# The down projection of a hybrid encoder layer: nine of 22 k-pairs with seven block products in place of eight

## The chip, the core and the metric

The kernel runs on one core of a Trainium2 chip. The metric is device time in microseconds (us) for one execution of the whole layer, and the comparison is between two kernels that compute the same layer.

## What is computed

One encoder layer over 256 tokens of 2048 channels, in float32: a windowed attention and a gated linear attention side by side, an output projection, and then a feed-forward part with a depthwise convolution of three taps. The change touches the last product alone, the one with `w_down`.

```python
D_MODEL, SEQ, D_FF = 2048, 256, 5632
def conv_gated_ffn(h, w_up, conv_w, conv_b, w_down):
    u = h @ w_up                                      # 256 x 11264
    up_ = jnp.pad(u, ((0, 0), (1, 1), (0, 0)))
    u = up_[:, :-2] * conv_w[0] + up_[:, 1:-1] * conv_w[1] + up_[:, 2:] * conv_w[2] + conv_b
    gate, val = jnp.split(u, 2, axis=-1)
    return (jax.nn.silu(gate) * val) @ w_down         # 256 x 5632 by 5632 x 2048
x = x + conv_gated_ffn(rms_norm(x, norm2_g), w_up, conv_w, conv_b, w_down)
```

## The kernel before

Every product of float32 numbers is made of three matmuls. A number is split into a rounded part (`hi`, type fp32r) and the residue (`lo`), and `hi*hi + hi*lo + lo*hi` is summed in PSUM. The activations are split once and stay in SBUF. The weights come from HBM unit by unit: `weights` (L104) loads 128x1024 numbers on SyncE's queue, ScalarE rounds them (L110) and VectorE subtracts to get the residue (L111). One unit is two k tiles of 128 rows by 512 output columns, and feeds 12 matmuls: two k tiles, two halves of 128 tokens, three matmuls each. The rings have four buffers for raw weights, four for `hi` and three for `lo`.

The program is recorded by a scheduler that fixes the order on every engine beforehand. An engine takes its instructions strictly in that order.

The up projection runs 22 chunks of eight units (`up`, L666). Each chunk's result leaves PSUM, is turned by a DMA, and goes through the convolution (`convolve`, L704) on VectorE and ScalarE while TensorE is already on later chunks; `behind` (L696) sets after which unit. So the convolution of the last two chunks, 20 and 21, runs while the down projection has begun. Their results are the split activations `gts`, 44 k tiles or 22 pairs of them.

The down projection (L733 to L761) takes the output columns in four blocks of 512. Each block runs over the 22 pairs, one unit a pair, into two PSUM banks (`pd`, one for each half of the tokens): 4 x 22 x 12 = 1056 matmuls. At the end of a block VectorE adds the two banks to `x1`, the input of the layer's last addition, and a DMA stores them. VectorE's residue of a unit has to wait until TensorE has let go of the `lo` buffer of three units before.

GpSimd has almost nothing to do before: twelve powers of a few columns (`inv_sqrt`, L188) and no work in the down projection.

Of the kernel before, what the change touches and what calls it, by code (L numbers as in the profile page):

```python
# [43 lines left out]
]  # L44

# [15 lines left out]
def tile_hymba_layer(  # L61
# [25 lines left out]
    def arena(shape, dt, name):  # L87
        return ar.tile(shape, dt, name=name, tag="ar")
# [644 lines left out]
    first = 0  # L733
    for c in range(4):
        ps = [acc(f"pd{c}{t}") for t in range(2)]
        for u in range(NFF // 2):
            hi, lo = weights(wd, first, 1024, f"d{c}{u}")
            if c == 0:
                behind(4 * NFF + u)
            first += P * 1024  # L740
            order = [(k, t) for k in range(2) for t in range(2)]
            if u == NFF // 2 - 1:
                order.sort(key=lambda o: o[1])
            for k, t in order:
                kt = 2 * u + k
                gt = gts[kt // 4]
                a = gt[:, 0, kt % 4, t * P : t * P + P]
                b = gt[:, 1, kt % 4, t * P : t * P + P]
                wh, wl = hi[:, k * 512 : k * 512 + 512], lo[:, k * 512 : k * 512 + 512]
                PE.matmul(ps[t], a, wh, start=(kt == 0), stop=False)  # L750
                PE.matmul(ps[t], a, wl, start=False, stop=False)  # L751
                PE.matmul(ps[t], b, wh, start=False, stop=(kt == NFF - 1))  # L752
        x1c = x1[c // 2][:, c % 2]
        for t in range(2):
            pieces = 2 if (c, t) == (3, 1) else 1
            w = 512 // pieces
            for i in range(pieces):
                sl = slice(i * w, i * w + w)
                V.tensor_tensor(x1c[:, t, sl], ps[t][:, sl], x1c[:, t, sl], ALU.add)
                q = nc.scalar if i == 0 and pieces == 2 else nc.sync  # L760
                q.dma_start(out=out[t * P : t * P + P, c * 512 + i * w : c * 512 + i * w + w], in_=x1c[:, t, sl])  # L761
# [106 lines left out]
```

## Time and profile before

| | us |
|---|---|
| median of 3 runs | 1063.92 (1063.69 to 1065.83) |
| the profiled execution, its own time | 1065.21 |
| its span, first to last instruction | 1063.4 |
| TensorE matmul busy | 1055.9 (99%) |
| VectorE busy | 703.7 (66%) |
| ScalarE busy | 581.7 (55%) |
| GpSimd busy | 15.2 (1%) |

The busy time of TensorE counts every moment in which some matmul is in flight. Matmuls overlap, so the distance between two starts is shorter than the length of one. The profiled execution's time holds 1.8 us outside its span. Its mean granted TensorE clock was 1.000, the full 2.4 GHz.

### The profile page before, as it was taken

How to read it: one execution, taken by the hardware profiler on the slowest of the kernel's cores; microseconds unless marked ns; L12 is line 12 of the kernel's file. 1: busy time of each engine (PE TensorE's matmuls, PEld its weight loads, DVE VectorE, ACT ScalarE, POOL GpSimd, SP SyncE). 2: the span in 40 equal slices, each digit the busy share in tenths (PEclk: the TensorE clock that was granted, in tenths of full speed). 3: DMA queues.
4: the chain of work that ended last, by engine and by line, in shares of the span. 5: the costliest groups of instructions: out<-in, count | busy, mean ns of one | idle time of the engine just before them, and what ended most of it. 6: DMA issues, size and time to landing. Idle time of an engine off the chain costs nothing.

```text
span 1063.4 us, 13494 instructions
## 1 busy us (share of the span) xinstructions
PE 1055.9 (99%) x4892; PEld 880.4 (83%) x4892; DVE 703.7 (66%) x957; ACT 581.7 (55%) x803; POOL 15.2 (1%) x16
## 2 busy tenths in 40 slices
PE   9999999999999999999999999999999999999998
PEld 7789888888888888888888888888888888888887
DVE  6598786755555567777777777777777755444543
ACT  6745686764445455656556565656556544433342
POOL 0021000010000000000000000000000000000000
PEclk9999999999999999999999999999999999999999
DMA  8955754346656797787887887788778767676762
GB/s 257 372 166 160 224 165 137 119 138 180 198 185 223 194 251 215 216 211 226 221 216 214 213 224 219 216 211 227 219 216 214 208 194 215 194 210 193 215 196 81
DMA packets 104706, 216.76 MB, mean 204 GB/s; under 512 B 53056, under 2 KB 53568, under 8 KB 104640
## 3 DMA queue, kind: packets, MB, share of 16 engines
q1 hardware_dynamic: 57888, 204.23, 62.8%
q10 hardware_dynamic: 46752, 11.68, 7.8%
q8 instruction: 38, 0.62, 0.2%
q14 instruction: 28, 0.23, 0.1%
HBM read 202.25 MB, written 2.10 MB: 192 GB/s over the span
## 4 chain that ended last, share of the span: by engine, by line
PE 95%; DMA 3%; DVE 1%; ACT 1%; issue 0%; DVEq 0%; SPq 0%; ACTq 0%
PE pu L678 15%; PE pu L677 15%; PE pu L679 15%; PE pd L752 8%; PE pd L750 7%; PE pd L751 7%; PE po L634 2%; PE po L635 2%; PE po L633 2%; PE pgt L259 1%; PE pqa L260 1%; PE pvg L260 1%; PE pvg L261 1%; PE pgt L261 1%; PE pgt L260 1%; PE pvg L259 1%
## 5 line engine op out<-in xcount | busy, mean ns | idle before, releaser
L111 DVE TENSOR_TENSOR lu<-ru,hu 128x1024 fp32r<-128x1024 f32 x176 | 215.1, 1222 | 124.8 <-PE pu L678 68.0
L679 PE MATMUL pu<-hu,xs 128*128 128x512 f32 x704 | 274.1, 389 | 0.0
L678 PE MATMUL pu<-lu,xs 128*128 128x512 f32 x704 | 273.9, 389 | 0.0
L677 PE MATMUL pu<-hu,xs 128*128 128x512 f32 x704 | 267.2, 389 | 0.0
L110 ACT ACTIVATE hu<-ru 128x1024 fp32r<-128x1024 f32 x176 | 186.8, 1061 | 145.7 <-PE pu L679 97.7
L111 DVE TENSOR_TENSOR ld<-rd,hd 128x1024 fp32r<-128x1024 f32 x88 | 107.7, 1224 | 112.5 <-PE pd L751 103.4
L110 ACT ACTIVATE hd<-rd 128x1024 fp32r<-128x1024 f32 x88 | 93.6, 1064 | 133.6 <-PE pd L752 128.2
L677 PEld LDWEIGHTS pu<-hu,xs 128*128 128x128 f32 x704 | 132.1, 188 | 27.5
L678 PEld LDWEIGHTS pu<-lu,xs 128*128 128x128 f32 x704 | 132.1, 188 | 27.4
L679 PEld LDWEIGHTS pu<-hu,xs 128*128 128x128 f32 x704 | 132.2, 188 | 27.4
L751 PE MATMUL pd<-ld,g 128*128 128x512 f32 x352 | 136.9, 389 | 0.0
L752 PE MATMUL pd<-hd,g 128*128 128x512 f32 x352 | 136.9, 389 | 0.0
L750 PE MATMUL pd<-hd,g 128*128 128x512 f32 x352 | 136.3, 389 | 0.0
L751 PEld LDWEIGHTS pd<-ld,g 128*128 128x128 f32 x352 | 66.1, 188 | 13.8
L752 PEld LDWEIGHTS pd<-hd,g 128*128 128x128 f32 x352 | 66.1, 188 | 13.7
L750 PEld LDWEIGHTS pd<-hd,g 128*128 128x128 f32 x352 | 66.1, 188 | 13.7
L111 DVE TENSOR_TENSOR lo<-ro,ho 128x1024 fp32r<-128x1024 f32 x32 | 38.8, 1223 | 39.0 <-ACT ho L110 29.1
L715 ACT ACTIVATE c<-v,prm_sb 128x256 f32<-128x256 f32 x88 | 48.2, 595 | 22.7 <-DVE c L719 19.5
L110 ACT ACTIVATE ho<-ro 128x1024 fp32r<-128x1024 f32 x32 | 33.9, 1060 | 46.9 <-DMA ro<-in_wo_dram 26.8
L716 DVE SCALAR_TENSOR_TENSOR c<-v,prm_sb,c 128x255 f32<-128x255 f32 x88 | 40.3, 478 | 0.6 <-ACT c L715 0.6
L685 ACT ACTIVATE us<-pu,rstd 128x512 f32<-128x512 f32 x44 | 29.9, 681 | 19.6 <-PE pu L679 19.6
L719 DVE SCALAR_TENSOR_TENSOR c<-v,prm_sb,c 128x255 f32<-128x255 f32 x88 | 40.2, 477 | 0.0
(215 smaller groups left out, 1432.6 us busy)
## 6 DMA issues: line engine op xcount, KB each, us to landing
ru<-in_wu_dram SPq DMA_DIRECT2D x176, 512.0 KB, 4.3
rd<-in_wd_dram SPq DMA_DIRECT2D x88, 512.0 KB, 4.4
ro<-in_wo_dram SPq DMA_DIRECT2D x32, 512.0 KB, 3.8
riqa<-in_wi_dram SPq DMA_DIRECT2D x16, 512.0 KB, 6.2
rivg<-in_wi_dram SPq DMA_DIRECT2D x16, 512.0 KB, 4.1
rigt<-in_wi_dram SPq DMA_DIRECT2D x16, 512.0 KB, 3.6
ri<-in_wi_dram SPq DMA_DIRECT2D x16, 384.0 KB, 4.1
riqg<-in_wi_dram SPq DMA_DIRECT2D x8, 512.0 KB, 5.0
```

The lines of the kernel that those rows point to most:

```text
L110: last["ACT"] = S.activation(hi[:, :cols], r[:, :cols], AF.Copy)
L111: last["DVE"] = V.tensor_tensor(lo[:, :cols], r[:, :cols], hi[:, :cols].bitcast(F32), ALU.subtract)
L260: PE.matmul(ps[t], xh, wl, start=False, stop=False)
L677: PE.matmul(ps[t], a, wh, start=(kt == 0), stop=False)
L678: PE.matmul(ps[t], a, wl, start=False, stop=False)
L679: PE.matmul(ps[t], b, wh, start=False, stop=(kt == NKT - 1))
L715: S.activation(c[:, j], v[:, j], AF.Identity, bias=cb[:, n : n + 1], scale=cw[:, 1, n : n + 1])
L716: V.scalar_tensor_tensor(out=c[:, j, 1:T], in0=v[:, j, 0 : T - 1], scalar=cw[:, 0, n : n + 1], in1=c[:, j, 1:T], op0=ALU.mult, op1=ALU.add)
L719: V.scalar_tensor_tensor(out=c[:, j, 0 : T - 1], in0=v[:, j, 1:T], scalar=cw[:, 2, n : n + 1], in1=c[:, j, 0 : T - 1], op0=ALU.mult, op1=A ...
L750: PE.matmul(ps[t], a, wh, start=(kt == 0), stop=False)
L751: PE.matmul(ps[t], a, wl, start=False, stop=False)
L752: PE.matmul(ps[t], b, wh, start=False, stop=(kt == NFF - 1))
```

## The change

The down projection now goes through the output columns in two halves of 1024, and through the 22 pairs in each half. A pair is a product of a 2x2 block matrix of activations (two halves of tokens by two k tiles) with a 2x2 block matrix of weights (two k tiles by two column blocks): eight block products, each 128 tokens by 128 k by 512 columns. For the nine pairs 1, 3, ..., 17 of each half these are replaced by Strassen's scheme in Winograd's form with seven. It needs sums of blocks. The four sums of weight blocks (`prepare`, four operations of 128x512) are made on GpSimd. The four sums of activation blocks of 128x128 and their split are made on VectorE and ScalarE. The seven block products need 3584 columns of split weights for the pair where two units have 2048 (`parts`: three operations of 1024 columns and one of 512, on ScalarE and on VectorE each). The products that enter more than one output go to four more PSUM banks (`pm`), and are added up after pair 17 on VectorE, ScalarE and GpSimd. The weights of such a pair are fetched by one DMA of 1 MB into `wraw`, two pairs ahead, and the sums are asked for one pair ahead; both have two buffers.

The pairs 0, 2, ..., 16 and 18 to 21 are computed as before, two units for each half. What is loaded from HBM is the same in size, reordered on the host.

```diff
-    first = 0
-    for c in range(4):
-        ps = [acc(f"pd{c}{t}") for t in range(2)]
-        for u in range(NFF // 2):
-            hi, lo = weights(wd, first, 1024, f"d{c}{u}")
-            if c == 0:
-                behind(4 * NFF + u)
...
+SEVEN = tuple(range(1, 18, 2))
...
+    def prepare(g):
+
+        b, ts = fetched[g]
+        b12, b11, b21, b22 = [b[:, i] for i in range(4)]
+        G.tensor_tensor(ts[:, 0], b12, b11, op=ALU.subtract)
+        G.tensor_tensor(ts[:, 3], b22, b12, op=ALU.subtract)
+        G.tensor_tensor(ts[:, 1], ts[:, 3], b11, op=ALU.add)
+        G.tensor_tensor(ts[:, 2], b21, ts[:, 1], op=ALU.subtract)
+        u = g % npair
+        gt, f = gts[u // 2], 2 * u % 4
+        a = work([P, 2, T], F32, f"ga{g}")
+        V.tensor_tensor(a, gt[:, 0, f : f + 2].bitcast(F32), gt[:, 1, f : f + 2].bitcast(F32), ALU.add)
+        a11, a12, a21, a22 = a[:, 0, 0:P], a[:, 1, 0:P], a[:, 0, P:T], a[:, 1, P:T]
+        c = work([P, 4, P], F32, f"gs{g}")
+        V.tensor_tensor(c[:, 0], a21, a22, ALU.add)
+        V.tensor_tensor(c[:, 1], c[:, 0], a11, ALU.subtract)
+        V.tensor_tensor(c[:, 2], a11, a21, ALU.subtract)
+        V.tensor_tensor(c[:, 3], a12, c[:, 1], ALU.subtract)
+        sp = work([P, 2, 4, P], F32R, f"gp{g}", "pT")
+        split(sp[:, 0], sp[:, 1], c)
+        sums[g] = sp
+
+    def parts(src, cols, name):
+        hi = wp.tile([P, WCOLS], F32R, name=f"h{name}", tag="hi", bufs=4)
+        lo = wp.tile([P, WCOLS], F32R, name=f"l{name}", tag="lo")
+        with tc.high_priority(offset=1500):
+            last["ACT"] = S.activation(hi[:, :cols], src, AF.Copy)
+            last["DVE"] = V.tensor_tensor(lo[:, :cols], src, hi[:, :cols].bitcast(F32), ALU.subtract)
+        return [(hi[:, i : i + 512], lo[:, i : i + 512]) for i in range(0, cols, 512)]
...
+            if (g + 2) % npair in SEVEN and g + 2 < 2 * npair:
+                fetch(g + 2)
+            if (g + 1) % npair in SEVEN and g + 1 < 2 * npair:
+                prepare(g + 1)
...
+                b11, b21 = parts(flat[:, 512:1536], 1024, f"d{g}a")
...
+                product(m1, gate(0, 0), b11, start=new, stop=end)
+                product(c11, gate(1, 0), b21, start=False, stop=False)
+                (b22,) = parts(flat[:, 1536:2048], 512, f"d{g}b")
+                product(c12, s4, b22, start=False, stop=False)
+                t1, t2 = parts(tflat[:, :1024], 1024, f"d{g}c")
...
+                product(m5, s1, t1, start=new, stop=end)
+                product(m6, s2, t2, start=new, stop=end)
+                t4, t3 = parts(tflat[:, 1024:], 1024, f"d{g}d")
+                product(c21, gate(1, 1), t4, start=False, stop=False)
+                product(m7, s3, t3, start=new, stop=end)
```

How the change moves instructions is shown at three places. The first is the end of GpSimd's program. Before, its last work is the power for the second norm (`rstd`):

```order
L188 TENSOR_TENSOR rk<-isq,mhalf 128x2 x2
L188 TENSOR_TENSOR rsq<-isq,mhalf 128x4 x4
L188 TENSOR_TENSOR rso<-isq,mhalf 128x2 x4
L188 TENSOR_TENSOR rstd_3187<-isq,mhalf 128x2
```

Now the sums of weights follow. A pair's weights `wraw` and sums `wsum` go to the buffers 7094 and 7096 for pair 1, to 7095 and 7097 for pair 3, to 7094 and 7096 again for pair 5, and so on:

```order
L192 TENSOR_TENSOR rstd_3187<-isq,mhalf 128x2
L755 TENSOR_TENSOR wsum_7096<-wraw_7094 128x512
L756 TENSOR_TENSOR wsum_7096<-wraw_7094 128x512
L757 TENSOR_TENSOR wsum_7096<-wsum_7096,wraw_7094 128x512
L758 TENSOR_TENSOR wsum_7096<-wraw_7094,wsum_7096 128x512
L755 TENSOR_TENSOR wsum_7096<-wraw_7094 128x512
L756 TENSOR_TENSOR wsum_7096<-wraw_7094 128x512
L757 TENSOR_TENSOR wsum_7096<-wsum_7096,wraw_7094 128x512
L758 TENSOR_TENSOR wsum_7096<-wraw_7094,wsum_7096 128x512
L755 TENSOR_TENSOR wsum_7097<-wraw_7095 128x512
L756 TENSOR_TENSOR wsum_7097<-wraw_7095 128x512
L757 TENSOR_TENSOR wsum_7097<-wsum_7097,wraw_7095 128x512
L758 TENSOR_TENSOR wsum_7097<-wraw_7095,wsum_7097 128x512
```

So four operations of 128x512 for each of the 18 pairs were added, 72 in all, and the scheduler has put those of pair 5 (rows 6 to 9) ahead of those of pair 3 (the last four).

The second place is VectorE in the second half of the columns, where nothing of the convolution is left. Before, only residues (`ld`) of units stand there, between two stores:

```order
L759 TENSOR_TENSOR x_2473<-pd_7095,x_2473 128x512
L111 TENSOR_TENSOR ld_7602<-rd_7599,hd_7601 128x1024
L111 TENSOR_TENSOR ld_7620<-rd_7617,hd_7619 128x1024
L111 TENSOR_TENSOR ld_7638<-rd_7635,hd_7637 128x1024
L111 TENSOR_TENSOR ld_7656<-rd_7653,hd_7655 128x1024
L111 TENSOR_TENSOR ld_7674<-rd_7671,hd_7673 128x1024
```

Now one round of two pairs, a product pair and a plain one, reads like this (`ld25a` to `ld25d` are the residues of pair 25, which is pair 3 of the second half; `gp`, `gs` and `ga` are activation sums for later pairs):

```order
L778 TENSOR_TENSOR ld25a<-wraw_7094,hd25a 128x1024
L131 TENSOR_TENSOR gp_8304<-gs_8299,gp_8304 128x512
L765 TENSOR_TENSOR gs_8563<-ga_8561 128x128
L767 TENSOR_TENSOR gs_8563<-ga_8561 128x128
L766 TENSOR_TENSOR gs_8563<-gs_8563,ga_8561 128x128
L778 TENSOR_TENSOR ld25b<-wraw_7094,hd25b 128x512
L768 TENSOR_TENSOR gs_8563<-ga_8561,gs_8563 128x128
L762 TENSOR_TENSOR ga_8649<-g_3198 128x512
L778 TENSOR_TENSOR ld25c<-wsum_7096,hd25c 128x1024
L778 TENSOR_TENSOR ld25d<-wsum_7096,hd25d 128x1024
L115 TENSOR_TENSOR ld_8310<-rd_8307,hd_8309 128x1024
L115 TENSOR_TENSOR ld_8328<-rd_8325,hd_8327 128x1024
```

In the place of four residues of 1024 columns a round has five and a half, and six operations for activation sums between them. Each of these instructions takes both its inputs from SBUF.

The third place is VectorE at the start of the down projection, with the convolution of chunk 20 (`v`, `c`) and the copies of chunk 21 (`pl`) between the residues. Before:

```order
L111 TENSOR_TENSOR ld_7099<-rd_7096,hd_7098 128x1024
L111 TENSOR_TENSOR ld_7117<-rd_7114,hd_7116 128x1024
L111 TENSOR_TENSOR ld_7135<-rd_7132,hd_7134 128x1024
L708 COPY v_7138<-uT_7017 128x2x512
L686 COPY pl_7087<-us_7086 128x1024
L708 COPY v_7147<-uT_7017 128x2x512
L686 COPY pl_7091<-us_7090 128x1024
L716 SCALAR_TENSOR_TENSOR c_7140<-v_7138,prm_sb,c_7140 128x255
L111 TENSOR_TENSOR ld_7175<-rd_7172,hd_7174 128x1024
```

Now:

```order
L115 TENSOR_TENSOR ld_7124<-rd_7121,hd_7123 128x1024
L115 TENSOR_TENSOR ld_7142<-rd_7139,hd_7141 128x1024
L778 TENSOR_TENSOR ld1a<-wraw_7094,hd1a 128x1024
L712 COPY v_7162<-uT_7017 128x2x512
L690 COPY pl_7087<-us_7086 128x1024
L690 COPY pl_7091<-us_7090 128x1024
L712 COPY v_7171<-uT_7017 128x2x512
L762 TENSOR_TENSOR ga_7111<-g_3192 128x512
L720 SCALAR_TENSOR_TENSOR c_7164<-v_7162,prm_sb,c_7164 128x255
L778 TENSOR_TENSOR ld1b<-wraw_7094,hd1b 128x512
L720 SCALAR_TENSOR_TENSOR c_7164<-v_7162,prm_sb,c_7164 128x255
L765 TENSOR_TENSOR gs_7113<-ga_7111 128x128
```

The third residue already belongs to pair 1 (`ld1a`), and the activation sums of pair 1 (`ga`, `gs`) have come in among the convolution.

## Rows read from the trace of the kernel before

**Rows 1.** The page: the busy line, and VectorE's line of the 40 slices.

```profile
PE 1055.9 (99%) x4892; PEld 880.4 (83%) x4892; DVE 703.7 (66%) x957; ACT 581.7 (55%) x803; POOL 15.2 (1%) x16
...
DVE  6598786755555567777777777777777755444543
```

**Rows 2.** Instructions on the tile `pd`: duration in ns, first and last start.

```profile
L750 PE MATMUL pd<-hd,g x352: 389/389/389, 820.2 to 1058.9; 128*128 128x512 f32 x176
...
L752 PE MATMUL pd<-hd,g x352: 388/389/389, 820.7 to 1059.4; 128*128 128x512 f32 x176
```

**Rows 3.** Who waited for whom, 820 to 1063 us: total, times, longest.

```profile
ACT hd L110 <- PE pd L752: 128.2, 79, 1.7
DVE ld L111 <- PE pd L751: 103.4, 72, 1.6
```

**Rows 4.** VectorE in order of time at the start of the down projection: start, length.

```profile
820.28 1.23 DVE L111 TENSOR_TENSOR ld<-rd,hd 128x1024 fp32r<-128x1024 f32 x1 [1.50 <-PE pu L678]
821.42 0.75 DVE L708 COPY v<-uT 128x1024 uint16<-128x1024 uint16 x1
822.06 0.68 DVE L686 COPY pl<-us 128x1024 uint16<-128x1024 uint16 x1
822.65 0.76 DVE L708 COPY v<-uT 128x1024 uint16<-128x1024 uint16 x1
...
825.42 0.48 DVE L716 SCALAR_TENSOR_TENSOR c<-v,prm_sb,c 128x255 f32<-128x255 f32 x1
825.82 0.48 DVE L719 SCALAR_TENSOR_TENSOR c<-v,prm_sb,c 128x255 f32<-128x255 f32 x1
```

**Rows 5.** Groups of VectorE and ScalarE by line and shape: count, busy, mean ns.

```profile
L111 DVE TENSOR_TENSOR ld<-rd,hd 128x1024 fp32r<-128x1024 f32 x88 | 107.7, 1224 | 112.5 <-PE pd L751 103.4 <-issue 5.1 <-PE pu L678 3.0
...
L724 DVE TENSOR_TENSOR c<-c,c 128x512 f32<-128x512 f32 x22 | 15.1, 686 | 0.1
...
L287 DVE TENSOR_TENSOR rope_kg<-cst_sb 128x128 f32<-128x128 f32 x8 | 1.7, 284 | 0.0
...
L110 ACT ACTIVATE hd<-rd 128x1024 fp32r<-128x1024 f32 x88 | 93.6, 1064 | 133.6 <-PE pd L752 128.2 <-PE pu L679 3.7 <-DVE c L716 1.7
...
L126 ACT ACTIVATE g<-c 128x512 fp32r<-128x512 f32 x22 | 13.9, 632 | 14.5 <-DVE c L724 14.5
```

**Rows 6.** GpSimd in order of time: start and length of its power operations.

```profile
46.85 0.70 POOL L188 TENSOR_TENSOR rstd<-isq,mhalf 128x2 f32<-128x2 f32 x1 [46.41 <-DVE isq L187]
...
69.58 3.24 POOL L188 TENSOR_TENSOR rsq<-isq,mhalf 128x4 f32<-128x4 f32 x1 [2.90 <-DVE isq L187]
74.22 1.45 POOL L188 TENSOR_TENSOR rsq<-isq,mhalf 128x4 f32<-128x4 f32 x1 [1.41 <-DVE isq L187]
...
87.31 1.38 POOL L188 TENSOR_TENSOR rsq<-isq,mhalf 128x4 f32<-128x4 f32 x1 [2.74 <-DVE isq L187]
```

**Rows 7.** VectorE in order of time beside these: start, length, operands.

```profile
69.41 0.42 DVE L298 TENSOR_TENSOR rsq<-qa_sb,rope_kg 128x256 f32<-128x256 f32 x1
69.74 0.68 DVE L304 TENSOR_TENSOR sqq<-qa_sb 128x512 f32<-128x512 f32 x1
70.35 1.00 DVE L111 TENSOR_TENSOR lilk<-rilk,hilk 128x816 fp32r<-128x816 f32 x1
71.27 0.68 DVE L299 TENSOR_TENSOR roq<-roq,rsq 128x512 f32<-128x512 f32 x1
71.87 0.68 DVE L305 TENSOR_REDUCE ssq<-sqq 128x4 f32<-128x512 f32 x1
...
74.39 0.42 DVE L298 TENSOR_TENSOR rsq<-qa_sb,rope_kg 128x256 f32<-128x256 f32 x1
74.72 0.68 DVE L127 TENSOR_TENSOR kvr<-ptk,kvr 128x512 fp32r<-128x512 f32 x1
...
87.14 0.69 DVE L299 TENSOR_TENSOR roq<-roq,rsq 128x512 f32<-128x512 f32 x1
```

More of the change, by code (lines that the diff above doesn't have):

```diff
@@ L610, in tile_hymba_layer @@
             store(ci, ps)
+    xs = [arena([P, 4, 2, T], F32R, f"xs{i}") for i in range(4)]
     x1 = [arena([P, 2, 2, 512], F32, f"x1{i}") for i in range(2)]
-    xs = [arena([P, 4, 2, T], F32R, f"xs{i}") for i in range(4)]
     ssq2 = pers.tile([P, 2, 4], F32, name="ssq2")
@@ L730, in tile_hymba_layer @@
         up(ch)
-    first = 0
-    for c in range(4):
-        ps = [acc(f"pd{c}{t}") for t in range(2)]
-        for u in range(NFF // 2):
-            hi, lo = weights(wd, first, 1024, f"d{c}{u}")
-            if c == 0:
-                behind(4 * NFF + u)
[L740 to L761, printed above, removed]
@@ new lines, in tile_hymba_layer, with fetch @@
+    npair = NFF // 2
+    wraw = [arena([P, 4, 512], F32, f"wraw{i}") for i in range(2)]
+    wsum = [arena([P, 4, 512], F32, f"wsum{i}") for i in range(2)]
+    fetched, sums = {}, {}
+    def fetch(g):
+        n = len(fetched)
+        fetched[g] = (wraw[n % 2], wsum[n % 2])
+        src = wd[g * P * 2048 : (g + 1) * P * 2048].rearrange("(p c) -> p c", p=P)
+        nc.sync.dma_start(out=wraw[n % 2].rearrange("p a c -> p (a c)"), in_=src)
+    def prepare(g):
[18 more added lines that the diff above has]
+        sums[g] = sp
@@ L830 @@
     w = a["w_down"][0]
-    wd = np.concatenate([_units(w[:, c * 512 : c * 512 + 512], [2] * (NFF // 2)) for c in range(4)])
+    w = w.reshape(NFF // 2, 2, P, 2, 2, 512)
+    blocks = []
+    for i in range(2):
+        for u in range(NFF // 2):
+            if u in SEVEN:
+                b = w[u, :, :, i]
+                blocks.append(np.stack([b[0, :, 1], b[0, :, 0], b[1, :, 0], b[1, :, 1]], 1).reshape(-1))
+            else:
+                blocks += [w[u, :, :, i, j].transpose(1, 0, 2).reshape(-1) for j in range(2)]
+    wd = np.concatenate(blocks)
     cos, sin, mask, mf, mb, dec = _constants()
```

52 lines of the change are left out of this document (added).

## The prediction, made before the changed kernel had run

> **What bounds the kernel now.** I read the page first. TensorE has a matmul in flight for 99% of the span, and VectorE, second, is at about seven tenths in the up projection and three to five tenths in the down projection [rows 1]. What a matmul of the down projection costs is the distance of starts and not its 389 ns: the first of 1056 starts at 820.2 us and the last at 1059.4 us [rows 2], which is 239.2 / 1055 = 0.2267 us each. Then the waits of this stage: ScalarE spends 128.2 us and VectorE 103.4 us waiting for TensorE to let go of weight buffers [rows 3], and TensorE waits for nobody. So removed matmuls count in full, as long as the engines that feed TensorE keep up. My sums are differences; I make them against the profiled execution (1065.21 us, 1.8 of it outside the span) and set them on the median of 1063.92, 1.3 us lower.
>
> **What is removed.** In each half nine pairs need 21 matmuls in place of 24: 2 x 9 x 3 = 54 matmuls, 54 x 0.2267 = 12.2 us. The end of the kernel (last bank, addition, store) is the same. HBM traffic is the same, and no queue ends a wait in rows 3, so I cost the DMAs at nothing; if fetches of 1 MB came late, the first matmuls of a product pair would wait for `wraw`.
>
> **What is added on ScalarE and VectorE.** I count a round, one plain pair and one product pair of a half. TensorE has 24 + 21 = 45 matmuls, 10.2 us. VectorE's instructions follow each other closer than they are long: 1.14 us for a residue of 1024 columns, 0.64 for a `v` copy, 0.59 for a `pl` copy, 0.40 for a convolution tap [rows 4], 0.60 for 512 columns (69.74 to 70.35) [rows 7], and 1.7 / 8 = 0.21 for 128x128 [rows 5]. A round has five residues of 1024 and one of 512 (6.3 us), and for the activations `ga` 0.60, four `gs` 0.84, and `gp` 0.60: 8.34 us. ScalarE has five roundings of 1.06 and two of 0.63, 6.6 us [rows 5]. Both fit under 10.2 us. With nothing else VectorE would have 1.9 us to spare in a round, the ring of three `lo` buffers would hold, and TensorE would not wait.
>
> **What is added on GpSimd.** Four operations of 128x512 with two inputs for each product pair, p us each. No such operation is in the trace. From below: VectorE does the shape in 0.69 us [rows 5]. From above: the smallest GpSimd operation takes 0.70 us [rows 6], and if both inputs are then read one after the other at VectorE's rate, (1.224 - 0.686) / 512 = 1.05 ns a column [rows 5], 2 x 0.54 is added: 1.77 us. I take 0.70 + 0.54 = 1.24, rounded to 1.2, the small GpSimd operation with VectorE's stream behind it, since a fixed part is what GpSimd's rows do show. The Trainium skill, in "GPSIMD Engine Reference" under "Performance versus the Vector engine", gives 4497 ns for an addition of 2048 columns; by that, scaled down, an estimate of p would be about 1.1 us, and the sum below some 6 us lower. No run so far shows it.
>
> Whether these 1.2 us lie beside VectorE's work is the question on which the forecast hangs, and here the trace speaks. GpSimd's powers have 128x2 or 128x4 inputs; undisturbed one takes 0.70 us. Next to a busy VectorE they took 3.24, 1.45 and 1.38 us [rows 6]. The 3.24 us one started at 69.58, while VectorE ran four operations back to back that take both inputs from SBUF, a residue (L111) among them; the last of the four ended at 71.95, and the power ended at 72.82, 0.87 later [rows 6, 7]. The one from 74.22 ended 0.86 us after the end (74.81) of the last operation of two SBUF inputs; the next VectorE operation, from 74.72, has one input in PSUM and did not hold it up. The one from 87.31 ended 0.86 us after 87.83, the end of L299 [rows 6, 7]. Three times the same rest, whatever went before: GpSimd gets nowhere while VectorE has two SBUF inputs, and does not slip in between back-to-back ones. Residues, `ga`, `gs` and `gp` are all of that kind.
>
> These rows show one direction. What a long GpSimd operation does to VectorE, no row shows, as the powers read only a few columns. The Trainium skill, in "SBUF — State Buffer" under "Who interferes with whom", says that the two share one pair of ports as an exclusive lock, and that a VectorE instruction with two SBUF inputs and a GpSimd instruction that reads SBUF block each other for the whole instruction, whichever started first. By that rule the work of both adds up, and the sum is the forecast's; by the rows alone, read as one direction, the sum is the second rival's.
>
> **The sum.** I take it that they exclude each other in both directions: the rows show a complete stop and no mere slowing, and what VectorE can withhold completely GpSimd must be using while it reads. First half, pairs 0 to 17, nine rounds: TensorE 405 x 0.2267 = 91.8 us. VectorE 9 x 8.34 = 75.1, and the convolution of chunks 20 and 21, each two `v` copies, eight taps, a product and a residue (5.7 us), and two `pl` copies: 11.4 + 1.2. That is 87.7, of which the copies (3.8) have one input and may lie beside GpSimd. GpSimd has eight pairs, 32 operations; the first pair's sums run under the last up chunk, where VectorE is at seven tenths [rows 1]. 87.7 - 3.8 + 32p = 83.9 + 32p, at p = 1.2 122.3: TensorE waits 30.5 us. Second half: by the order some activation sums are made earlier, under the four plain pairs that close the first half, so VectorE has about 71; two pairs of weight sums are also ahead, 28 operations are left: 71 + 28p = 104.6, and TensorE waits 12.8 us. Together +43.3 - 12.2 = +31 us: 1065.2 + 31 = 1096 for a profiled execution, **1095 us** against the median.
>
> The additions after pair 17 (five VectorE operations of 0.60, one of ScalarE) lie under the four plain pairs, where TensorE has 21.8 us and VectorE needs 9. The four banks of the next half are freed under the last 12 matmuls of this one. I cost them at nothing; without that cover they are 2 to 3 us.
>
> **Bounds.** p = 0.69: 14.2 + 0 - 12.2 = +2, 1066 us. p = 1.77: 48.7 + 28.8 - 12.2 = +65, 1129 us. The gain is eaten up when 83.9 + 32p - 91.8 = 12.2, at p = 0.63, less than VectorE itself needs.
>
> **Rivals.** (1) *Handovers on top.* A weight sum goes from GpSimd to ScalarE (1.06 us) to VectorE, each in strict order. If TensorE has run dry, each of 17 product pairs pays one rounding that nothing covers, 17 x 1.06 = 18 us: 1113. For it: GpSimd has pair 5 ahead of pair 3, and pair 5's sums wait for `ld1d` to free their buffer, so pair 3's come late. Against: while ScalarE rounds the first two sums, GpSimd's fourth can run.
>
> (2) *Faster: a GpSimd operation under way holds nobody up.* Then it needs only a moment to start, its 1.2 us lie beside VectorE, and rounds run at TensorE's 10.2 us. It decides from the point where VectorE's idle moments in a round (1.9 us) suffice for four starts. The trace neither shows nor excludes it. What is left is the start: from `ld1a` to the residue `ld21` of pair 2 the order has 16.0 us of VectorE work (four residues of 1024 and one of 512 after the first 1.14, the convolution of chunk 20, two sets of sums), from 820.3 on. TensorE comes to `ld21` after 59 matmuls, 13.4 us after 820.2. So 2.7 us are lost there, and about half as much again at chunk 21: 1063.9 - 12.2 + 4 = 1056 us.
>
> (3) *Cheap sums.* They exclude each other, but a GpSimd operation reads for only 0.7 to 0.85 us of its time: 1066 to 1074 us by the same sum.
>
> The granted clock was 1.000 with a TensorE that never paused; no row shows what pauses of some us do to it. A fall to 1.2 GHz would add to any of the waits.
>
> **How the numbers follow.** My forecast (1074 to 1106) 0.45; rival 1 and dearer sums (above 1106) 0.17; rival 3 0.13; rival 2 (1052 to 1061) 0.25. The likeliest is 1095, and its own range is 1066 to 1129. With rival 2 in, the range goes from 1054, which leaves out a little of rival 2, to 1125, which leaves out the dearest sums; together under 2 in 10. What a measurement of this kernel can tell from no change is about 0.2%, 2 us. Faster is rival 2, 0.25. Same, 1062 to 1066, is the edge of rivals 2 and 3, 0.05. Slower 0.70.
>
> **What would show it.** Removed matmuls: 4838 on TensorE in place of 4892, still 0.2267 us apart inside a unit. Exclusion: GpSimd operations of 128x512 of very different lengths, short ones where VectorE pauses, long ones that end a fixed time after a VectorE operation; VectorE residues that start late with no releaser shown; waits of TensorE for `hd` and `ld` of product pairs, and of ScalarE for `wsum`. Rounds of some 13 us in the first half and 12 in the second in place of 10.2. It is wrong if rounds last 10.2 us with GpSimd operations of 1.2 us beside residues of 1.22, if GpSimd's operations are much longer or shorter than 1.2 us when alone, or if TensorE waits for `wraw`.

## The result, and the profile after

The changed kernel takes 1102.09 us (median of 4 runs, 1100.31 to 1102.5), the one before in the same runs 1063.81 (1063.2 to 1065.83). The ratio is 1.0354, with an interval of 1.0339 to 1.037: 38 us slower. The forecast was 1095 in a range of 1054 to 1125. The profiled execution took 1102.41 us by its own time, with a span of 1100.6.

The page after, to be read against [rows 1]: busy time, then VectorE's and GpSimd's lines of the 40 slices and the granted clock.

```profile
PE 1064.8 (97%) x4838; PEld 875.2 (80%) x4838; DVE 843.9 (77%) x1111; ACT 620.1 (56%) x859; POOL 173.3 (16%) x94
...
DVE  6598786656456487777777776777699989999986
...
POOL 0030000000000000000000000000024697625631
PEclk9999999999999999999999999999998999999999
```

The 54 matmuls are gone. VectorE's slices, three to five tenths in the down projection before, now mostly read nine, although only some 150 instructions were added there. Where the down projection lost time is read from the starts of matmuls on a few tiles. The first two rows hold the first and the last start of the stage; `ld17d` ends the product pairs of the first half, and `hd23a` and `ld39d` are the first and last product pair of the second.

```profile
L135 PE MATMUL pd<-hd,g x208: 386/389/628, 819.0 to 1095.8; 128*128 128x512 f32 x104
...
L137 PE MATMUL pd<-hd,g x208: 388/389/628, 819.4 to 1096.3; 128*128 128x512 f32 x104
...
L136 PE MATMUL pm<-ld17d,gp x1: 396/396/396, 944.4 to 944.4; 128*128 128x512 f32 x1
...
L135 PE MATMUL pm<-hd23a,g x1: 389/389/389, 972.0 to 972.0; 128*128 128x512 f32 x1
...
L136 PE MATMUL pm<-ld39d,gp x1: 389/389/389, 1074.5 to 1074.5; 128*128 128x512 f32 x1
```

In the order on TensorE, 404 distances of 0.2267 us lie between the first and the third of these starts, 103 to the fourth, 398 to the fifth and 96 to the last: 91.6, 23.3, 90.2 and 21.8 us without waiting. The rows show 125.4, 27.6, 102.5 and 21.8. So 33.8 us are lost in the first half, 4.2 in and around its four plain pairs, 12.3 in the second half, and nothing at the end: 50.3 us. 12.2 are saved and the stage began 1.2 us earlier (819.0 against 820.2), which makes +36.9; the spans differ by 37.2.

Next the groups of GpSimd and VectorE by shape, 815 to 1100 us (count, busy, mean ns, idle before). VectorE's rows answer to [rows 5].

```profile
L755 POOL TENSOR_TENSOR wsum<-wraw 128x512 f32<-128x512 f32 x17 | 49.3, 2899 | 102.7 <-DMA wraw<-in_wd_dram 74.2 <-DVE c L720 18.8 <-DVE gs L768 9.7
L756 POOL TENSOR_TENSOR wsum<-wraw 128x512 f32<-128x512 f32 x17 | 31.2, 1836 | 1.8 <-DVE ld5d L778 1.8
...
L115 DVE TENSOR_TENSOR ld<-rd,hd 128x1024 fp32r<-128x1024 f32 x52 | 74.3, 1450 | 2.9 <-PE pd L136 1.7 <-issue 1.2
...
L765 DVE TENSOR_TENSOR gs<-ga 128x128 f32<-128x128 f32 x18 | 11.7, 650 | 0.1
...
L778 DVE TENSOR_TENSOR ld31a<-wraw,hd31a 128x1024 fp32r<-128x1024 f32 x1 | 2.3, 2316 | 0.0
```

A residue was 1224 ns and is 1450 on the mean; `gs` of 128x128 has 650 where the shape had 284; some residues of 1024 columns take 2.3 us. The same work has become longer. Two stretches show how. GpSimd in order of time, start and length, first beside `ld31a`, then beside a VectorE that is behind:

```profile
1019.48 1.40 POOL L755 TENSOR_TENSOR wsum<-wraw 128x512 f32<-128x512 f32 x1 [5.97 <-DMA wraw<-in_wd_dram]
1020.83 2.29 POOL L756 TENSOR_TENSOR wsum<-wraw 128x512 f32<-128x512 f32 x1
...
883.03 16.79 POOL L755 TENSOR_TENSOR wsum<-wraw 128x512 f32<-128x512 f32 x1 [9.70 <-DVE gs L768]
899.79 1.33 POOL L756 TENSOR_TENSOR wsum<-wraw 128x512 f32<-128x512 f32 x1
901.20 1.26 POOL L757 TENSOR_TENSOR wsum<-wsum,wraw 128x512 f32<-128x512 f32 x1
```

And VectorE at the same places:

```profile
1019.64 2.32 DVE L778 TENSOR_TENSOR ld31a<-wraw,hd31a 128x1024 fp32r<-128x1024 f32 x1
1021.88 1.79 DVE L131 TENSOR_TENSOR gp<-gs,gp 128x512 fp32r<-128x512 f32 x1
...
898.38 0.29 DVE L766 TENSOR_TENSOR gs<-gs,ga 128x128 f32<-128x128 f32 x1
898.71 1.26 DVE L768 TENSOR_TENSOR gs<-ga,gs 128x128 f32<-128x128 f32 x1
903.58 1.31 DVE L778 TENSOR_TENSOR ld11c<-wsum,hd11c 128x1024 fp32r<-128x1024 f32 x1 [3.60 <-ACT hd11c L777]
```

Read the two together. `ld31a` starts 0.16 us after a GpSimd sum and takes 2.32 us, 1.10 more than alone. The next sum starts inside `ld31a`, cannot go on until it ends at 1021.96, and ends at 1023.12, 1.16 us later; `gp`, issued at 1021.88, takes 1.79, 1.10 more than the 0.69 of its shape. Here the two engines take turns, and neither works while the other has its turn. From 882.87 to 898.67 VectorE had 25 operations back to back, each with two SBUF inputs and each at its usual length. The sum of pair 11 got nowhere for 15.6 us and ended 1.15 us after that chain; then `gs`, due at 0.28 us, took 1.26. With VectorE standing still (3.60 us before `ld11c`), a sum takes 1.26 us.

Directly behind it stands the other pattern. VectorE, then GpSimd:

```profile
907.04 4.54 DVE L115 TENSOR_TENSOR ld<-rd,hd 128x1024 fp32r<-128x1024 f32 x2
911.51 2.31 DVE L778 TENSOR_TENSOR ld13a<-wraw,hd13a 128x1024 fp32r<-128x1024 f32 x1
...
908.34 2.16 POOL L757 TENSOR_TENSOR wsum<-wsum,wraw 128x512 f32<-128x512 f32 x1
910.58 2.16 POOL L758 TENSOR_TENSOR wsum<-wraw,wsum 128x512 f32<-128x512 f32 x1
```

From 904.93 to 921.66 us VectorE again shows no gap, but here GpSimd got a turn before each of its eight operations, and each is about 1.1 us longer than usual. So GpSimd was held off for a whole chain in one place and let in after every operation in another; what decides between the two, no run shows.

The waits that answer to [rows 3], 815 to 1100 us: total, times, longest.

```profile
POOL wsum L755 <- DMA wraw<-in_wd_dram: 74.2, 11, 24.4
...
PE pd L136 <- DVE ld L115: 9.2, 6, 2.4
...
ACT hd11c L777 <- POOL wsum L757: 6.7, 1, 6.7
```

TensorE, which waited for nobody, now waits for VectorE's residues and for much else in small pieces. VectorE's waits for TensorE, 103.4 us for residues before, are 13 us in all, and ScalarE's, 128.2 before, are some 80.

### The profile page after: what moved, and what is told of

The parts are those of the page before. It is cut to its first block, busy times and chain, and to the rows that moved or that the text cites. A ratio compares the mean times of both kernels' runs of the same rounds, so it can differ in the third digit from the quotient of the medians.

```text
span 1100.6 us, 13710 instructions
## 1 busy us (share of the span) xinstructions
PE 1064.8 (97%) x4838; PEld 875.2 (80%) x4838; DVE 843.9 (77%) x1111; ACT 620.1 (56%) x859; POOL 173.3 (16%) x94
## 4 chain that ended last, share of the span: by engine, by line
PE 82%; DVE 9%; DMA 3%; issue 2%; POOL 2%; ACT 1%; DVEq 0%; ACTq 0%
PE pu L681 15%; PE pu L682 14%; PE pu L683 14%; PE pd L136 4%; PE pd L137 4%; PE pd L135 4%; DMA ro<-in_wo_dram 2%; PE po L638 2%; PE po L639 2%; PE po L637 2%; POOL wsum L755 2%; PE pgt L263 1%; PE pqa L264 1%; PE pvg L265 1%; PE pvg L264 1%
## 5 line engine op out<-in xcount | busy, mean ns | idle before, releaser
L114 ACT ACTIVATE hu<-ru 128x1024 fp32r<-128x1024 f32 x176 | 186.5, 1060 | 144.4 <-PE pu L683 96.1
L755 POOL TENSOR_TENSOR wsum<-wraw 128x512 f32<-128x512 f32 x18 | 51.9, 2882 | 560.9 <-PE pu L683 458.2
L136 PE MATMUL pd<-ld,g 128*128 128x512 f32 x208 | 83.6, 402 | 9.3 <-DVE ld L115 9.2
L137 PE MATMUL pd<-hd,g 128*128 128x512 f32 x208 | 82.8, 398 | 0.0
L135 PE MATMUL pd<-hd,g 128*128 128x512 f32 x208 | 76.9, 403 | 1.2 <-ACT hd L114 1.2
L115 DVE TENSOR_TENSOR ld<-rd,hd 128x1024 fp32r<-128x1024 f32 x52 | 74.3, 1450 | 2.9 <-PE pd L136 1.7
L115 DVE TENSOR_TENSOR lo<-ro,ho 128x1024 fp32r<-128x1024 f32 x32 | 38.9, 1224 | 39.3 <-ACT ho L114 29.5
L114 ACT ACTIVATE hd<-rd 128x1024 fp32r<-128x1024 f32 x52 | 53.7, 1055 | 23.1 <-PE pd L137 15.0
L136 PEld LDWEIGHTS pd<-ld,g 128*128 128x128 f32 x208 | 40.0, 193 | 21.0 <-DVE ld L115 12.5
L135 PEld LDWEIGHTS pd<-hd,g 128*128 128x128 f32 x208 | 40.3, 195 | 11.4 <-ACT hd L114 2.8
L137 PEld LDWEIGHTS pd<-hd,g 128*128 128x128 f32 x208 | 40.1, 193 | 8.2
L723 DVE SCALAR_TENSOR_TENSOR c<-v,prm_sb,c 128x255 f32<-128x255 f32 x88 | 44.6, 525 | 0.0
L720 DVE SCALAR_TENSOR_TENSOR c<-v,prm_sb,c 128x255 f32<-128x255 f32 x88 | 44.4, 526 | 0.0
```

Of the source, the lines that this page charges most:

```text
L114: last["ACT"] = S.activation(hi[:, :cols], r[:, :cols], AF.Copy)
L115: last["DVE"] = V.tensor_tensor(lo[:, :cols], r[:, :cols], hi[:, :cols].bitcast(F32), ALU.subtract)
L135: PE.matmul(d, a[0], b[0], start=start, stop=False)
L136: PE.matmul(d, a[0], b[1], start=False, stop=False)
L137: PE.matmul(d, a[1], b[0], start=False, stop=stop)
L720: V.scalar_tensor_tensor(out=c[:, j, 1:T], in0=v[:, j, 0 : T - 1], scalar=cw[:, 0, n : n + 1], in1=c[:, j, 1:T], op0=ALU.mult, op1=ALU.add)
```

## The experiments

Three theories stood against each other. T1: a GpSimd operation that reads SBUF and a VectorE operation with two SBUF inputs shut each other out, and the work of both adds up. T2: it is the handovers between engines or their order (rival 1). T3: VectorE alone, with its new work and the convolutions at the start, is the bound. Beside the medians I use one stretch that the convolutions don't touch, from `hd23a` to `ld39d` of the second half: 102.5 us in the changed kernel.

**Without the sums.**

```diff
-        G.tensor_tensor(ts[:, 0], b12, b11, op=ALU.subtract)
-        G.tensor_tensor(ts[:, 3], b22, b12, op=ALU.subtract)
-        G.tensor_tensor(ts[:, 1], ts[:, 3], b11, op=ALU.add)
-        G.tensor_tensor(ts[:, 2], b21, ts[:, 1], op=ALU.subtract)
...
-                t1, t2 = parts(tflat[:, :1024], 1024, f"d{g}c")
+                t1, t2 = parts(flat[:, :1024], 1024, f"d{g}c")
...
-                t4, t3 = parts(tflat[:, 1024:], 1024, f"d{g}d")
+                t4, t3 = parts(flat[:, 1024:], 1024, f"d{g}d")
```

> GpSimd's four weight sums of each product pair are left out; the residues and roundings that read them read the fetched weights in their place, so TensorE, VectorE and ScalarE keep all their instructions. Theory 1 (GpSimd and two-input VectorE operations exclude each other): 54 matmuls saved and only the start's backlog lost, 1056 us (1052 to 1062), residues of 1.22 us throughout. Theory 2 (handovers from GpSimd to ScalarE to VectorE and their order): the same, 1052 to 1062, as there is nothing to hand over. Theory 3 (VectorE's new residues and activation sums alone are too much): 1075 or more.

Measured: 1065.05 us (one run), between the expectations. Its two tile rows give 946.9 to 1037.2, 90.3 us:

```profile
L135 PE MATMUL pm<-hd23a,g x1: 389/389/389, 946.9 to 946.9; 128*128 128x512 f32 x1
...
L136 PE MATMUL pm<-ld39d,gp x1: 389/389/389, 1037.2 to 1037.2; 128*128 128x512 f32 x1
```

The 398 distances take what they take without waiting: without GpSimd nothing is lost in the second half, T1's point. But 13.1 us are lost in the first (the stage begins at 818.4, `ld17d` comes at 923.1, and 404 distances are 91.6), nearly all at the start, where VectorE stood in a wait that I had not seen. Waits of VectorE and for VectorE, 818 to 862 us:

```profile
DVE gs L761 <- DMA uT<-pl: 5.4, 1, 5.4
...
PE pd L137 <- DVE gp L131: 4.6, 1, 4.6
```

The activation sums `gs` take a buffer of the ring in which the evicted planes `pl` of chunk 21 lie, and one of these was still being read by the DMA that turns them. VectorE keeps its order, and stood for 5.4 us with residues queued behind. That this wait is most of the 13.1 us is not shown by this run; the experiment with another ring, below, takes it away in another version.

**Fills in the place of sums.**

```diff
...
+        for k in (0, 3, 1, 2):
+            G.memset(ts[:, k], 0.0)
```

> GpSimd's four weight sums are replaced by four fills of the same tiles with zero (so the weight sums are left out of the result): GpSimd still writes 128x512 four times a pair and ScalarE and VectorE still wait for it, but it reads nothing. Theory 1: if the exclusion is about reading, VectorE's residues stay at 1.22 us and the time is 1053 to 1064 us; if it is about writing too, some 1085 to 1105. Theory 2: the handovers are all there, 1080 or more with residues of 1.22 us. Theory 3: 1075 or more.

Measured: 1059.95 us (one run), and 90.3 us from `hd23a` to `ld39d`. GpSimd's fills, then the activation sums `gp` of VectorE in the changed kernel and in this one:

```profile
L756 POOL MEMSET wsum<- x72: 522/528/535, 803.5 to 1010.7; 128x512 f32 x72
...
L131 DVE TENSOR_TENSOR gp<-gs,gp 128x512 fp32r<-128x512 f32 x18 | 23.1, 1286 | 0.0
...
L131 DVE TENSOR_TENSOR gp<-gs,gp 128x512 fp32r<-128x512 f32 x18 | 12.3, 686 | 0.0
```

Every handover from GpSimd to ScalarE to VectorE is there, and costs nothing: T2 falls in this form. The time by itself doesn't tell whether fills exclude VectorE, since 28 of 0.53 us would fit into the second half: 71 + 15 is under 91.8 us. The lengths do. All 72 fills took 522 to 535 ns, and `gp` has 686 ns as without GpSimd, where it has 1286 beside sums: what excludes VectorE is GpSimd's reading. Here `gs` did not wait for the turned chunk, and the first half lost 7.0 us (819.5 to 918.1) in place of 13.1.

**The sums on VectorE** (`G.tensor_tensor` becomes `V.tensor_tensor` in the four lines).

> The four weight sums are made on VectorE. Theory 1: a sum costs the shared resource 0.60 us in place of 1.27, and 32 x 0.6 stand in the first half against a VectorE that has 87.7 us for TensorE's 91.8: 15 us lost there, nothing in the second half (71 + 16.8 = 87.8), so 1064 - 12 + 15 = 1067 us (1060 to 1074). Theory 2: the handover to ScalarE and back is still there, 1085 or more. Theory 3: 1100 or more, as VectorE gets more work.

Measured: 1078.2 us (1076.95 to 1080.37), ratio 1.0143 (1.0128 to 1.0158). Faster than GpSimd by 24 us, but 4 us above my range. From `hd23a` to `ld39d` it takes 92.2 us, so VectorE carries the sums nearly for nothing there. The miss is the first half: some 24 us are lost up to `ld17d`, against 15 expected and 33.8 with GpSimd. `gs` waits 5.3 us for the turned chunk again, in two pieces, and the clock falls to 0.75 between 830 and 860.

**GpSimd in the order of pairs.**

```diff
...
+        if "POOL" in last:
+            in_order(i1, last["POOL"])
+            in_order(i2, last["POOL"])
...
```

> GpSimd's sums are held in the order of the pairs, so that pair 3 no longer stands behind pair 5. Theory 1: the sum of work is the same, 1096 to 1104 us. Theory 2: the late sums of pair 3 are what starves TensorE, 10 us or more are won back, below 1092. Theory 3: no change, 1100 to 1104.

Measured: 1106.15 us (1100.55 to 1107.66), ratio 1.0411 (1.0394 to 1.0428), not better than with pair 5 ahead of pair 3, and 2 us above T1's range. T2's other form falls. Why four of its five runs are 4 to 6 us above the changed kernel stays open: the profile is of the fifth, 1100.55 us.

**One more sum for each pair.**

```diff
         G.tensor_tensor(ts[:, 2], b21, ts[:, 1], op=ALU.subtract)
+        G.tensor_tensor(ts[:, 2], b21, ts[:, 1], op=ALU.subtract)
```

> The changed kernel with the last of GpSimd's four sums (L758) made twice, so that a product pair has five operations of 128x512 on GpSimd in place of four; the result is the same. T1 (GpSimd's reading and VectorE's two-input operations shut each other out, so the work of both adds up where TensorE already waits): an operation alone takes 1.27 us, 18 more of them, of which those for the first pair of each half lie under work with slack, so 15 to 17 x 1.27 = +19 to +22 us, 1121 to 1124 us; VectorE busy grows too, as its operations are stretched. T2 (a fixed price for each handover from GpSimd to ScalarE to VectorE): the number of handovers is the same, so under +5 us. T3 (VectorE's own load and the fallen clock are the loss): no change, 1100 to 1104.

Measured: 1119.61 us (1118.18 to 1121.84), ratio 1.0527 (1.0511 to 1.0543), so +17.5.

```profile
L136 PE MATMUL pm<-ld17d,gp x1: 389/389/389, 953.8 to 953.8; 128*128 128x512 f32 x1
...
L135 PE MATMUL pm<-hd23a,g x1: 389/389/389, 981.5 to 981.5; 128*128 128x512 f32 x1
...
L136 PE MATMUL pm<-ld39d,gp x1: 389/389/389, 1091.9 to 1091.9; 128*128 128x512 f32 x1
```

How many sums of GpSimd lie between the first start and `ld17d`, in the changed kernel and here (busy time and count of what touches `wsum` on VectorE, ScalarE and GpSimd, then clock, DMA share and GB/s):

```profile
819.00:944.40 125.40, 26.71 (x18) 19.03 (x18) 82.02 (x36) 0.93 0.48 154
...
818.70:953.80 135.10, 29.94 (x18) 19.11 (x18) 100.18 (x45) 0.91 0.46 144
```

From the first start (818.7) to `ld17d` it takes 135.1 us, 9.7 more than the changed kernel, for nine operations; over the four plain pairs 27.7, as before; from `hd23a` to `ld39d` 110.4, 7.9 more for seven. That is 17.6 / 16 = 1.10 us for each, under the 1.27 that I expected, and the same 1.10 by which the neighbours were stretched above. T2 and T3, which gave under 5 us or no change, fall.

**The second half alone** (product pairs `range(23, 40, 2)`, sums on GpSimd).

> Product pairs in the second half of the columns alone (pairs 1, 3, ..., 17 of it), sums on GpSimd as in the changed kernel; the first half is plain throughout, the result is the same. Saved: 27 matmuls x 0.2267 = 6.1 us. T1 (mutual exclusion, 28 operations that nothing covers): the loss of the second half as the changed kernel has it, 12.8 us, so 1063.8 - 6.1 + 12.8 = 1070.5 us (1067 to 1074), with TensorE's clock at 1.00 until the second half. T3 (the loss starts with VectorE's backlog at the convolutions, and the later loss is its echo): nothing is lost, 1057 to 1060. No rounds of more than 11 us by T3, 11 to 12.5 us by T1.

Measured: 1074.01 us (1072.92 to 1075.1), ratio 1.01 (1.0084 to 1.0116). From `hd23a` to `ld39d` 942.7 to 1045.2, 102.5 us, the changed kernel's number to the tenth, though nothing was late before: T3's echo of the start falls. It came out at the upper edge of my range for one more reason of T1's kind: GpSimd made eight sums ahead, at 844 to 859 us, beside the convolutions, and TensorE ran 117 matmuls in 830 to 860 where 134 fit, 3.9 us. Together 1063.8 - 6.1 + 12.3 + 3.9 = 1073.9.

**Late pairs, GpSimd against VectorE.** Product pairs 8, 10, ..., 16 in the first half, after the convolutions, and 1, 3, ..., 17 in the second.

```diff
+PAIRS = (8, 10, 12, 14, 16) + tuple(range(23, 40, 2))
```

> The late version (product pairs 8, 10, ..., 16 and 1, 3, ..., 17 of the second half, two buffers each) with the weight sums on GpSimd as in the changed kernel in place of VectorE; same result. Without GpSimd it took 1058.6 us. It has no product pair beside the convolutions, so that a difference is GpSimd's alone. T1 (the work of the two adds up): a round is 8.34 + 4 x 1.27 = 13.4 us against TensorE's 10.2; second half 12.5 us lost as in the version with the second half alone, four rounds of the first half at 2 to 3.2 us, so 1063.8 - 9.5 + 12.5 + 8 to 13 = 1075 to 1080. T2 (a price of 1.06 us for each handover from GpSimd to ScalarE, 14 pairs): 1067 to 1072. T3 (GpSimd costs nothing where VectorE isn't behind already; in the changed kernel it was behind from the start): 1054 to 1058.

> Product pairs 8, 10, 12, 14, 16 in the first half of the columns, after the convolutions of chunks 20 and 21, and 1, 3, ..., 17 in the second; the weight sums on VectorE, nothing on GpSimd. The result is the same. Saved: 14 x 3 = 42 matmuls, 9.5 us. A round of two pairs has 10.2 us on TensorE and 8.34 + 4 x 0.60 = 10.74 on VectorE, with some sums made ahead under plain pairs. T1 (the start is where VectorE's sums are late; elsewhere it just keeps up): 1054 to 1058, clock 1.00 throughout. T3 (10.74 against 10.2 us in every round is lost in full, 14 x 0.54 = 7.6, and pauses bring the clock down): 1060 to 1066.

Measured: 1079.0 us (1077.98 to 1079.81) with the sums on GpSimd, ratio 1.0132 (1.0108 to 1.0155), and 1058.6 (1057.52 to 1060.31) on VectorE, 0.9953 (0.994 to 0.9966), between its two expectations. Only the engine of 56 operations differs. Of the 20 us, 4 still lie beside the convolutions: GpSimd made its first eight sums there, from 846 to 861 us, and 850 to 880 has 114 starts of matmuls in place of 132. The busy times by stretch (length; TensorE, its weight loads, VectorE, ScalarE and GpSimd, each with its count of operations; clock; DMA share and GB/s), first of the version on GpSimd, then of that on VectorE:

```profile
865.00:925.00 60.00, 58.08 (x251) 46.35 (x250) 58.26 (x43) 33.59 (x37) 38.13 (x21) 1.00 0.62 196
...
945.00:1035.00 90.00, 82.62 (x349) 65.60 (x348) 85.43 (x74) 47.19 (x52) 47.48 (x27) 0.98 0.57 187
```

```profile
865.00:925.00 60.00, 59.98 (x264) 49.26 (x264) 57.83 (x72) 33.74 (x37) 5.63 (x3) 1.00 0.62 207
...
945.00:1035.00 90.00, 87.42 (x383) 71.21 (x382) 84.12 (x110) 52.69 (x58) 1.29 (x1) 1.00 0.55 179
```

VectorE is as busy in both (85.43 and 84.12 of 90 us). With the sums on GpSimd the two engines together get 74 + 27 operations done, without it VectorE alone 110, and TensorE 383 matmuls in place of 349. The busy time of VectorE counts the time that it is held up inside an operation, so it hides the loss. The idle engine's help made the busy one slower than doing all of it itself.

**Three buffers for the fetch.** The late version on VectorE lost some 3 us at 945 us. Its wait there:

```profile
DVE wsum L755 <- DMA wraw<-in_wd_dram: 3.6, 1, 3.6
```

The fetch of 1 MB can begin only when `wraw` of two product pairs before is free.

```diff
-    wraw = [arena([P, 4, 512], F32, f"wraw{i}") for i in range(2)]
-    wsum = [arena([P, 4, 512], F32, f"wsum{i}") for i in range(2)]
+    wraw = [arena([P, 4, 512], F32, f"wraw{i}") for i in range(3)]
+    wsum = [arena([P, 4, 512], F32, f"wsum{i}") for i in range(1)]
...
-            if (g + 2) % npair in SEVEN and g + 2 < 2 * npair:
-                fetch(g + 2)
+            if g + 4 in PAIRS:
+                fetch(g + 4)
```

> The late version (product pairs 8, 10, ..., 16 and 1, 3, ..., 17 of the second half, sums on VectorE) with three buffers for the fetched weights in place of two and one for their sums in place of two, and fetches four pairs ahead in place of two; same result, same SBUF. In the late version TensorE lost some 3 us at 945 us, where VectorE stood 3.6 us for a fetch of 1 MB that could start only when the buffer of two product pairs before was free. T1 (that wait is the loss): no wait of VectorE for the fetch, 1054.5 to 1057. T3 (VectorE's 10.74 us in a round of 10.2 are the loss): as before, 1057.5 to 1060. If the one buffer for sums makes VectorE wait instead: above 1060.

Measured: 1055.8 us (1055.02 to 1056.18), ratio 0.9924 (0.9911 to 0.9936). VectorE no longer waits for a fetch at 945 us. It beats both kernels, 8 us under the one before, and 1.5 above what 42 matmuls save.

**Every third pair, VectorE and GpSimd** (2, 5, ..., 17 of each half).

> Six product pairs in each half, every third pair (2, 5, ..., 17) in place of nine, and the weight sums on VectorE; nothing on GpSimd. The result is the same. Saved: 36 matmuls x 0.2267 = 8.2 us. A round of three pairs has 69 matmuls, 15.6 us, and VectorE has 2 x 2.28 + 4.02 + 2.04 + 4 x 0.60 = 13.0 us, so it fits away from the start. T1 (what is left without GpSimd is the start, where the convolutions of chunks 20 and 21 share VectorE with the first product pairs): second half without loss, some 4 to 10 us lost before 860 us, 1060 to 1066. T3 (VectorE can't keep up with sums at all): rounds longer than 16 us all along, above 1070.

> Every third pair (2, 5, ..., 17) with the weight sums on GpSimd as in the changed kernel; same result. It saves 36 matmuls, 8.2 us. A round of three pairs has 15.6 us on TensorE, and VectorE 10.6 + GpSimd 4 x 1.27 = 15.7 us. T1 (the work of the two adds up, and costs nothing as long as the sum stays under TensorE's time): outside the start nothing or little is lost although GpSimd's operations are stretched beside VectorE's; with a loss at the start of 14 to 22 us, 1069 to 1078. T2 (each of 12 product pairs pays for its handover, 1.06 us and more): 13 us or more on top, above 1080. T3 (only VectorE's own load counts, GpSimd is free): faster than the version with the sums on VectorE (1069.3), as VectorE has 2.4 us less a round.

Measured: 1069.31 us (1068.61 to 1069.62) on VectorE, ratio 1.0051 (1.0038 to 1.0065), above my range; 1078.61 (1078.42 to 1079.27) on GpSimd, 1.0139 (1.0124 to 1.0155), 0.6 above T1's range. Of the difference of 9.3 us, 34 matmuls (7.7 us) are lost between 830 and 900 us and 6 (1.4 us) between 930 and 970, where the halves meet. From 970 to 1060 us TensorE has 134 matmuls in each 30 us, as many as the kernel before, with GpSimd's operations stretched between:

```profile
970.00:1000.00 30.00, 30.00 (x134) 24.85 (x133) 25.93 (x22) 15.70 (x17) 15.33 (x8) 1.00 0.59 194
```

So the two engines' work still adds up, as GpSimd's 15.33 us for eight operations show, but the sum fits under TensorE's round.

**Another ring for the activation sums**, in the version with every third pair on VectorE.

```diff
-        a = work([P, 2, T], F32, f"ga{g}")
+        a = work([P, 2, T], F32, f"ga{g}", "sc", 3)
...
-        c = work([P, 4, P], F32, f"gs{g}")
+        c = work([P, 4, P], F32, f"gs{g}", "sc", 3)
```

> Every third pair (2, 5, ..., 17) with the sums on VectorE, 1069.3 us so far, with the activation sums ga and gs in the ring of three buffers of the convolution in place of the ring of four that the evicted chunk's planes use; same result. In the version with every third pair VectorE stood 5.24 us at the gs of pair 5, whose buffer was still being read by the DMA that turns chunk 21, with the convolution and the residues queued behind it, and the granted clock was 0.90 in 830 to 860 us. T1 (this wait for a buffer, in strict order, is most of the loss at the start): the wait is gone or shorter, TensorE gains 5 to 10 us there, 1059 to 1064. T3 (VectorE's sheer backlog beside the convolutions is the loss): the wait moves to another place and the time stays at 1067 to 1070.

Measured: 1063.26 us (1062.5 to 1064.04), 6.0 less, ratio 0.9995 (0.9986 to 1.0004). The wait of VectorE for the turned chunk is gone, and 830 to 860 us reads, before this edit and after it:

```profile
830.00:860.00 30.00, 23.25 (x83) 16.49 (x82) 24.76 (x44) 13.70 (x17) 0.00 (x0) 0.90 0.57 180
```

```profile
830.00:860.00 30.00, 28.94 (x123) 22.44 (x123) 29.78 (x44) 18.12 (x22) 0.00 (x0) 1.00 0.67 220
```

123 matmuls in place of 83, at a clock of 1.00 in place of 0.90, with VectorE now busy throughout. What is still lost, 31 matmuls up to 900 us (7.0 us), is VectorE's backlog beside the convolutions, so both T1's and T3's reason hold here, about half each.

## Why the prediction was right

**The matmuls.** 54 fewer, 12.2 us: as predicted.

**Exclusion, in both directions.** The forecast hung on it, and it held. GpSimd stood for 15.6 us beside back-to-back VectorE operations, the direction that [rows 6, 7] had shown; VectorE's residues were stretched by 1.10 us, the direction that no row had shown. The Trainium skill, in "SBUF — State Buffer" under "Who interferes with whom", has it as a lock that whoever comes first holds for a whole instruction; the rows at 1019 to 1023 us agree, each engine ending one whole operation after the other's. The rows at 883 us don't agree with whoever comes first: GpSimd's sum stood from 883.03, and 24 operations that VectorE started later went ahead of it. The profile shows the stretch not as residues that start late, as I had put it, but as residues that are longer, inside the busy time. Rival 2 (a sum under way holds nobody up, 1056 us) falls by the late pair of kernels, 1079.0 against 1058.6.

**The price p.** I took 1.2 us from bounds of 0.69 and 1.77. Alone a sum takes 1.26 to 1.33; as an addition to a waiting round, 1.10. Rival 3 had GpSimd reading for only 0.70 to 0.85 us of it, and falls with 1.10. The Trainium skill's figure in "GPSIMD Engine Reference" under "Performance versus the Vector engine", scaled to an estimate of 1.1 us, was near; for the length of a sum alone the trace's 1.26 decides.

**First half.** Predicted 30.5 us lost, measured 33.8. The sum 83.9 + 32p, which then is 91.8 + 33.8 = 125.6, would ask for p = 1.30, more than any other measure here. The count was wrong: 36 sums lie in this stretch, as the sums of pair 23, which I took off the second half as made ahead, run from 936.0 to 942.7 us, before `ld17d`. 83.9 + 36p = 125.6 gives p = 1.16. VectorE is busy for all but 5.7 us of it, 3.6 of these before `ld11c`: the stage is set by the two engines' turns. The wait for the turned chunk's buffer, 5.4 us without GpSimd, does not add to this, since in the changed kernel VectorE comes to `gs` so late that the buffer is free.

**The four plain pairs.** I let them hide the additions and all that is made ahead for nothing; 4.2 us were lost. Here a step failed. I had 28 operations left in the second half because eight were made ahead, and charged the stretches where they were made with nothing: four fell into the first half, four here; and of the additions after pair 17 I counted VectorE's five and ScalarE's one, and not the three on GpSimd. The trace has seven GpSimd operations from 944.4 to 957.2 us, and VectorE without a pause from 944.9 to 970.3. In the version without sums this stretch (923.1 to 946.9) lost 0.5.

**Second half.** Predicted 12.8 us lost, measured 12.3, which is p = 1.18; four kernels with different first halves took 102.5 to 103.1 from `hd23a` to `ld39d`, against 90.3 without the sums.

**Rival 1**, dear handovers and pair 5 ahead of pair 3, falls by the fills and by the kernel in the order of pairs. What it had right is mainly one, `hd11c`, 6.7 of the 16 us that ScalarE waited for GpSimd, behind the sum that VectorE kept out.

**The sum.** 30.5 + 0 + 12.8 - 12.2 = +31 predicted; 33.8 + 4.2 + 12.3 - 12.2 - 1.2 = +37 measured. What is missing comes from the eight sums made ahead that were charged nowhere: 3.3 us in the first half (four more at 1.2, less 1.4 because p was 1.16) and the plain pairs (4.2). But for that 1.4 the two misses don't cancel, so the number's being near owes little to luck.

**What stays open.** GpSimd waited 74.2 us for `wraw`. I took none of that for a loss, since the second half's sum came out without it; three buffers were tried only with the sums on VectorE, where they gave 2.8 us. How much of the start is the fallen clock by itself no run separates, nor what lets GpSimd in between VectorE's operations at 905 us and not at 883.

## What to carry to other kernels

An idle GpSimd is no free place for elementwise work with SBUF inputs while VectorE works on two SBUF inputs: add both engines' times for the stage, at 1.1 to 1.2 us for 128x512 here, and compare the sum with the time of the engine that sets the stage. Here VectorE did the same operation in 0.60 us, so that putting the sums on the busy engine was better by 24 us. Then look at what a moved or added operation's buffer shares a ring with, for in a strict order one late buffer stops all that is queued behind it; and start a scheme that needs the second engine only after its busiest stretch.

## What the runs showed of the hardware that was not expected

The granted clock fell after TensorE had paused, which no row of the kernel before could show. Stretches of the changed kernel, with TensorE first and the clock after GpSimd's count; from 861 to 863 us no matmul ran, and right behind it the clock fell:

```profile
829.00:836.00 7.00, 5.18 (x14) 3.16 (x12) 7.00 (x6) 1.33 (x2) 6.36 (x5) 0.76 0.00 0
...
861.00:863.00 2.00, 0.00 (x0) 0.00 (x0) 2.00 (x3) 0.05 (x1) 1.92 (x2) 1.00 0.27 115
863.00:865.00 2.00, 1.53 (x4) 1.24 (x5) 2.00 (x3) 0.00 (x0) 2.00 (x2) 0.60 0.00 0
...
870.00:900.00 30.00, 27.29 (x113) 20.85 (x114) 29.94 (x47) 15.18 (x19) 20.22 (x4) 1.00 0.54 176
```

TensorE had only 14 matmuls in the 7 us in which the clock stood at 0.76, a mix of its two levels, 2.4 and 1.2 GHz, and a matmul of 389 ns then took 628. VectorE is busy for the whole of these stretches, which speaks for a small cost of the clock by itself. In the second half two kernels show it: from `hd23a` to `ld39d` the changed kernel had a mean clock of 0.98 and the one with the second half alone 1.00, and both took 102.5 us. In the version with the sums on VectorE the clock fell to 0.75 in 830 to 860 us, with GpSimd idle, so the fall doesn't need GpSimd.

VectorE can hold GpSimd off for a whole chain: a sum of 1.26 us lasted 16.79. It doesn't always, as the turns from 904.93 us show. A GpSimd operation that only writes, a fill of 0.53 us, did not disturb VectorE measurably (`gp` 686 ns). And VectorE's operations with one input in PSUM ran at their usual 0.68 us while GpSimd read. VectorE, then GpSimd, whose turn came when the residue ended at 949.39:

```profile
949.31 0.68 DVE L824 TENSOR_TENSOR ut<-pm,us 128x512 f32<-128x512 f32 x1
949.91 0.68 DVE L828 TENSOR_TENSOR x<-pm,x 128x512 f32<-128x512 f32 x1
...
948.38 2.16 POOL L757 TENSOR_TENSOR wsum<-wsum,wraw 128x512 f32<-128x512 f32 x1
```
